# The mixture-of-experts stage of a Hyena layer: one 512-column matmul for both parts of the tokens, in 13 of 16 experts

## The chip, the cores and the metric

The kernel runs on one NeuronCore of a Trainium2 chip. The metric is the device time of one execution in microseconds (us), the median of three runs. TensorE is shown as PE (matmuls) and PEld (weight loads), VectorE as DVE, ScalarE as ACT, GpSimd as POOL, and SyncE, which issues the weight transfers, as SP.

## What is computed

One post-norm layer: a bidirectional Hyena long convolution over 2048 tokens of width 1024, then an expert-choice mixture of 16 experts. The change is in the experts alone:

```python
def _expert_choice_moe(h, w_router, w1, w3, w2):
    cap = EC_CAPACITY * T // N_EXPERTS          # 256 tokens for each expert
    aff = jax.nn.softmax((h @ w_router).astype(F32), -1)
    gate, idx = lax.top_k(jnp.swapaxes(aff, 1, 2), cap)
    xe = h[bidx, idx]
    he = jax.nn.silu(jnp.einsum('becd,edf->becf', xe, w1)) * jnp.einsum('becd,edf->becf', xe, w3)
    ye = jnp.einsum('becf,efd->becd', he, w2) * gate[..., None].astype(h.dtype)
    return jnp.zeros_like(h).at[bidx, idx].add(ye)
```

d is 1024 and f is 2048. All weights are fp32, 24 MB for an expert.

## The kernel before

Everything in fp32 is done by splitting: a number is a rounded part (h, "high") plus a remainder (l, "low"), each in a format that TensorE takes in one pass (fp32r), and a product a*b is three matmuls that add into the same place of PSUM: ah*bh, ah*bl, al*bh (`mm3`, L174, whose matmuls stand on L175, L176 and L177). In the profile's names `ab<-xh,w1h` the output is `ab`, the moving operand (streamed through the array, one column after the other) `xh`, and the stationary one (loaded first) `w1h`.

The stage of the experts is `phase_moe`. Each expert has 256 tokens. `route` (L1436) finds their indices, gathers the 256 rows (`xg`), transposes them on TensorE into PSUM (`tp`) four times 4 tiles, and splits each `tp` into `xh` (ACT, L1469) and `xl` (DVE, L1470). The 2048 hidden features are done in 16 blocks of 128: eight slices of weights (`fc`), and in each two blocks (`i`). For a slice, `load` brings w1, w3 and w2 (1 MB each) by SP's queue and `split` makes their high and low parts (ACT L1385, DVE L1386). For a block:

- `project` (L1479): 8 steps of k for w1 and 8 for w3. Each step is one `mm3` with 256 moving columns, so a block has 48 matmuls of 256 columns. w1's result and w3's are the two halves of one PSUM bank `ab` (2 buffers).
- `hidden` (L1489): Silu of the first half (ACT, L1491), times the second half (DVE, L1492), split into `hh` (ACT, L170) and `hl` (DVE, L171).
- `back` (L1498): 12 matmuls of 512 columns that add hidden times w2 into four banks `acc`. It is put off by one block: `flush` issues the `back` of block n-1 behind the `project` of block n, so that ACT and DVE have the time of a `back` and a `project` to make `hh` and `hl`.

After an expert's last block `finish` weighs the four `acc` banks (DVE, `y`, L1509) and scatters them into `accd` in HBM by an indirect DMA of POOL (L1515); `y` has one buffer, so that the second half of the tokens waits until the first half's DMA has landed.

Experts 0 to 12 run in the loop on L1570; there the framework's scheduler orders each engine's instructions. Experts 13 to 15 run in the loop on L1596 under a manual schedule (the order as written), together with `settle` (L1517), which normalises rows of `accd` that are complete and writes them out; it borrows the buffers of `xh` and `xl` for that. PSUM has 8 banks: four `acc`, two `ab`, two `tp`.

Of the kernel before, what the change touches and what calls it, by code (L numbers as in the profile page):

```python
# [12 lines left out]
F32 = mybir.dt.float32  # L13
F32R = mybir.dt.float32r
# [3 lines left out]
AF = mybir.ActivationFunctionType  # L18
# [31 lines left out]
def f_(ap):  # L50
    return ap.bitcast(F32)
# [122 lines left out]
def mm3(nc, out, ah, al, bh, bl, start=True, stop=True):  # L174
    nc.tensor.matmul(out, lhsT=ah, rhs=bh, start=start, stop=False)  # L175
    nc.tensor.matmul(out, lhsT=ah, rhs=bl, start=False, stop=False)  # L176
    nc.tensor.matmul(out, lhsT=al, rhs=bh, start=False, stop=stop)  # L177
# [1247 lines left out]
def phase_moe(tc, A, rowd, ident, ones_f, lg, R, xnd, accd, out):  # L1425
    nc = tc.nc
    tab, lo, hi, slot, spf = R.tab, R.lo, R.hi, R.slot, R.spf
    with ExitStack() as st:
# [7 lines left out]
        def route(e):  # L1436
# [4 lines left out]
            yield  # L1441
            p = ps.tile([128, 2, 33], F32, name="tp")
            idx = wk.tile([128, 2], I32, name="idx", bufs=4)
# [15 lines left out]
            yield  # L1459
            xh = wk.tile([128, 8, 256], F32R, name="xh")  # L1460
            xl = wk.tile([128, 8, 256], F32R, name="xl")
            nxt[:] = [idx, gate, xh, xl]
            for q in range(4):
                p = ps.tile([128, 2, 256], F32, name="tp")
                for i in range(2):
                    k = 2 * q + i
                    for h in range(2):
                        nc.tensor.transpose(out=p[:, i, h * 128:h * 128 + 128], in_=xg[h][:, k * 128:k * 128 + 128], identity=ident)
                nc.scalar.copy(xh[:, 2 * q:2 * q + 2], p)  # L1469
                nc.vector.tensor_tensor(xl[:, 2 * q:2 * q + 2], p, f_(xh[:, 2 * q:2 * q + 2]), OP.subtract)  # L1470
                yield
# [6 lines left out]

        def project(i, x, ws):  # L1479

            xh, xl = x
            fs = slice(i * 128, i * 128 + 128)
            p = ps.tile([128, 2, 256], F32, name="ab")
            for j in range(2):
                for k in range(8):
                    mm3(nc, p[:, j], ws[2 * j][:, k, fs], ws[2 * j + 1][:, k, fs], xh[:, k], xl[:, k], start=(k == 0), stop=(k == 7))
            return p

        def hidden(p):  # L1489
            s = wk.tile([128, 256], F32, name="s")  # L1490
            nc.scalar.activation(s, p[:, 0], AF.Silu)  # L1491
            nc.vector.tensor_tensor(s, s, p[:, 1], OP.mult)  # L1492
            hh = wk.tile([128, 256], F32R, name="hh")
            hl = wk.tile([128, 256], F32R, name="hl")
            split_const(nc, hh, s, hl)
            return hh, hl
# [19 lines left out]

        def settle(name, idx=None):  # L1517


            x = wk.tile([128, 2, 1024], F32, name=name)  # L1520
            if idx is None:
# [48 lines left out]
        for e in range(NE - 3):  # L1570
            idx, gate, *x = nxt
            acc = [[pa.tile([128, 512], F32, name=f"acc{h}{q}") for q in range(2)] for h in range(2)]
# [18 lines left out]
        with tc.manual_schedule():  # L1591
# [4 lines left out]
            for e in range(NE - 3, NE):  # L1596
                prev = acc, idx, gate
                idx, gate, *x = nxt
                acc = [[pa.tile([128, 512], F32, name=f"acc{h}{q}") for q in range(2)] for h in range(2)]
                rt = iter(()) if e == NE - 1 else route(e + 1)  # L1600
                for n in range(16):
                    fc, i = divmod(n, 2)
                    if i == 0:
                        ws, nw = nw, []
                    p = project(i, x, ws)
                    flush()
# [14 lines left out]
                    if todo:  # L1621
                        act.append(settle(todo[-2:], prev[1] if todo[0] == "-" else None))
                        next(act[-1])
# [10 lines left out]
            flush()  # L1634
            ys = [wk.tile([128, 1024], F32, name=n) for n in ("xh", "xl")]

# [130 lines left out]
```

## Time and profile before

| | |
|---|---|
| median of 3 runs | 4205.35 us (4202.3 to 4205.91) |
| the profiled execution | 4207.69 us, of which the profiled span is 4205.7 us |
| TensorE matmul, share of the span | 93% |
| mean granted TensorE clock | 0.967 of full speed |
| first matmul of the experts' blocks | at 1943.5 us of the span |
| the small matmuls of `route` (L1449) in expert 12, half-way through it | at 3673.3 us |

The profile's page gives each engine's busy time, the clock and traffic in 40 slices, the chain of work that ended last (followed back from the end through whatever released each step), and the costliest groups of instructions. Matmuls are pipelined and the ends of their records are modelled: one lasts longer in the records than the next one's start. What a matmul takes of TensorE's time is therefore the distance from its start to the next one's start, read from the timeline.

### The profile page before, as it was taken

What the parts mean: (1) busy time and instruction counts of PE and PEld (TensorE: products, weight loads), DVE (VectorE), ACT (ScalarE), POOL (GpSimd) and SP (SyncE); (2) the same over time, 40 slices, a digit from 0 to 9 for tenths busy, and PEclk for the clock granted to TensorE, in tenths of its full rate; (3) what the DMA queues carried; (4) which work ended last, traced back from release to release, by engine and by line L of the source; (5) the groups of instructions that cost most, each with busy time, mean ns of one, the idle gap of its engine ahead of it and who ended that gap; (6) DMA issues with size and microseconds to landing.
All of it is one profiled execution on the core that took longest, in us unless ns stands there. A gap on an engine that the chain in (4) does not pass through costs nothing.

```text
span 4205.7 us, 59336 instructions
## 1 busy us (share of the span) xinstructions
PE 3916.2 (93%) x23158; PEld 3360.2 (80%) x23158; DVE 2623.2 (62%) x3636; ACT 1886.3 (45%) x2609; POOL 961.1 (23%) x918
## 2 busy tenths in 40 slices
PE   6788999999998987965999999999999999999997
PEld 2445787787777776755999999999999999998996
DVE  7997444776766766876555555555555555556666
ACT  4554332334876873122444444444444444444443
POOL 4674211222332342120000000000000000005635
PEclk7999999999999999987999999999999999999999
DMA  6665445666778776543566666666566656656664
GB/s 188 189 203 177 129 153 174 206 212 194 208 208 230 208 222 205 166 165 123 189 213 201 191 190 201 200 191 201 192 209 194 204 193 209 193 171 228 225 230 166
DMA packets 648180, 815.30 MB, mean 194 GB/s; under 512 B 51411, under 2 KB 543203, under 8 KB 645596
## 3 DMA queue, kind: packets, MB, share of 16 engines
q1 hardware_dynamic: 593442, 694.82, 52.3%
q0 software_dynamic: 37472, 113.86, 9.3%
q10 hardware_dynamic: 16986, 2.83, 0.4%
q8 instruction: 182, 2.98, 0.3%
q14 instruction: 98, 0.80, 0.1%
HBM read 627.04 MB, written 133.97 MB: 181 GB/s over the span
## 4 chain that ended last, share of the span: by engine, by line
PE 74%; DVE 10%; DMA 8%; issue 4%; POOL 3%; ACT 1%; SPq 0%; POOLq 0%; DVEq 0%; ACTq 0%
PE ab L175 10%; PE ab L177 10%; PE ab L176 10%; PE acc L175 5%; PE acc L176 5%; PE acc L177 5%; PE ip L175 4%; PE ip L177 4%; PE ip L176 4%; DMA xr<-s1o 3%; PE xp L853 1%; PE op L175 1%; PE op L177 1%; PE op L176 1%; PE xp L833 1%
## 5 line engine op out<-in xcount | busy, mean ns | idle before, releaser
L177 PE MATMUL ab<-xh,w1l 128*128 128x256 f32 x2048 | 581.5, 284 | 3.2 <-DVE w1l L1386 3.0
L175 PE MATMUL ab<-xh,w1h 128*128 128x256 f32 x2048 | 582.9, 285 | 0.0
L177 PE MATMUL ab<-xh,w3l 128*128 128x256 f32 x2048 | 579.7, 283 | 0.5 <-DVE w3l L1386 0.5
L176 PE MATMUL ab<-xl,w1h 128*128 128x256 f32 x2048 | 579.8, 283 | 0.0
L176 PE MATMUL ab<-xl,w3h 128*128 128x256 f32 x2048 | 579.6, 283 | 0.0
L175 PE MATMUL ab<-xh,w3h 128*128 128x256 f32 x2048 | 579.6, 283 | 0.0
L1386 DVE TENSOR_TENSOR w2l<-w2r,w2h 128x2048 fp32r<-128x2048 f32 x126 | 297.6, 2362 | 317.6 <-ACT w2h L1385 317.6
L175 PE MATMUL acc<-w2h,hh 128*128 128x512 f32 x1024 | 405.4, 396 | 14.0 <-ACT hh L170 13.5
L176 PE MATMUL acc<-w2l,hh 128*128 128x512 f32 x1024 | 403.3, 394 | 0.0
L177 PE MATMUL acc<-w2h,hl 128*128 128x512 f32 x1024 | 400.5, 391 | 0.8 <-DVE hl L171 0.8
L175 PEld LDWEIGHTS ab<-xh,w1h 128*128 128x128 f32 x2048 | 392.5, 192 | 8.8 <-ACT xh L1469 0.3
L176 PEld LDWEIGHTS ab<-xl,w1h 128*128 128x128 f32 x2048 | 392.4, 192 | 8.6
L177 PEld LDWEIGHTS ab<-xh,w1l 128*128 128x128 f32 x2048 | 392.2, 191 | 4.2 <-DVE w1l L1386 4.2
L177 PEld LDWEIGHTS ab<-xh,w3l 128*128 128x128 f32 x2048 | 393.2, 192 | 0.9 <-DVE w3l L1386 0.9
L176 PEld LDWEIGHTS ab<-xl,w3h 128*128 128x128 f32 x2048 | 393.2, 192 | 0.0
L175 PEld LDWEIGHTS ab<-xh,w3h 128*128 128x128 f32 x2048 | 393.1, 192 | 0.0
L1492 DVE TENSOR_TENSOR s<-s,ab 128x256 f32<-128x256 f32 x256 | 106.9, 417 | 399.6 <-ACT s L1491 399.5
L1386 DVE TENSOR_TENSOR w1l<-w1r,w1h 128x2048 fp32r<-128x2048 f32 x126 | 301.0, 2389 | 69.5 <-ACT w1h L1385 69.4
L1386 DVE TENSOR_TENSOR w3l<-w3r,w3h 128x2048 fp32r<-128x2048 f32 x126 | 292.9, 2325 | 53.8 <-ACT w3h L1385 53.8
L1515 POOL DMA_INDIRECT accd<-y,idx x27 | 64.4, 2385 | 1120.2 <-DVE y L1509 1120.2
L1385 ACT CAST w2h<-w2r 128x2048 fp32r<-128x2048 f32 x128 | 244.0, 1906 | 153.3 <-PE acc L177 145.1
L1491 ACT ACTIVATE s<-ab 128x256 f32<-128x256 f32 x256 | 97.4, 380 | 448.0 <-PE ab L177 448.0
(401 smaller groups left out, 8728.1 us busy)
## 6 DMA issues: line engine op xcount, KB each, us to landing
w1r<-in_moe_w_dram SPq DMA_DIRECT2D x128, 1024.0 KB
w3r<-in_moe_w_dram SPq DMA_DIRECT2D x128, 1024.0 KB
w2r<-in_moe_w_dram SPq DMA_DIRECT2D x128, 1024.0 KB
fud<-ev SPq DMA_DIRECT2D x128, 256.0 KB
kr<-fud SPq DMA_DIRECT2D x64, 512.0 KB
mw<-in_mod_w_dram SPq DMA_DIRECT2D x96, 256.0 KB
wraw<-in_hy_w_in_dram SPq DMA_DIRECT2D x48, 512.0 KB
win<-in_c_win_dram SPq DMA_DIRECT2D x64, 256.0 KB
```

The source lines that it names most:

```text
L175: nc.tensor.matmul(out, lhsT=ah, rhs=bh, start=start, stop=False)
L176: nc.tensor.matmul(out, lhsT=ah, rhs=bl, start=False, stop=False)
L177: nc.tensor.matmul(out, lhsT=al, rhs=bh, start=False, stop=stop)
L833: nc.tensor.matmul(p[:, i], lhsT=s2[:, 2 * gp + i], rhs=r[:, i], start=True, stop=True)
L853: nc.tensor.matmul(p[:, i], lhsT=s2[:, 2 * gp + i], rhs=r[:, i], start=True, stop=True)
L1385: nc.scalar.copy(h, raw)
L1386: eng.tensor_tensor(l, raw, f_(h), OP.subtract)
L1491: nc.scalar.activation(s, p[:, 0], AF.Silu)
L1492: nc.vector.tensor_tensor(s, s, p[:, 1], OP.mult)
L1515: nc.gpsimd.indirect_dma_start(out=accd, out_offset=at(idx, h), in_=y, in_offset=None, compute_op=OP.add)
```

## The change

In experts 0 to 12 the high and the low parts of the tokens stand side by side in one tile `xs` (for each k: 256 columns high, 256 low). `project` now gives w1 and w3 a PSUM bank each. A step of k is two matmuls: the weights' high part against all 512 columns of `xs` (L1487), and the weights' low part against the 256 high columns (L1488), which adds into the first half of the bank. The two halves of a bank are then summed: ACT copies the second half to SBUF (L1490, `u0` or `u1`), DVE adds the first half (L1491). Silu (ACT, L1493) and the product of `u0` and `u1` (DVE, L1510) now read SBUF. `ab` has three buffers, and `tp` one.

Experts 13 to 15 keep the 256-column products and one bank (`project_summed`, L1497), reading both halves of `xs`. `settle` gets its buffers from a tile `xs`, which is taken at an expert's start.

```diff
@@ route
-            p = ps.tile([128, 2, 33], F32, name="tp")
+            p = ps.tile([128, 2, 33], F32, name="tp", bufs=1)
...
-            xh = wk.tile([128, 8, 256], F32R, name="xh")
-            xl = wk.tile([128, 8, 256], F32R, name="xl")
-            nxt[:] = [idx, gate, xh, xl]
+            xs = wk.tile([128, 8, 2, 256], F32R, name="xs")
+            nxt[:] = [idx, gate, xs]
             for q in range(4):
-                p = ps.tile([128, 2, 256], F32, name="tp")
+                p = ps.tile([128, 2, 256], F32, name="tp", bufs=1)
...
-                nc.scalar.copy(xh[:, 2 * q:2 * q + 2], p)
-                nc.vector.tensor_tensor(xl[:, 2 * q:2 * q + 2], p, f_(xh[:, 2 * q:2 * q + 2]), OP.subtract)
+                xh, xl = (xs[:, 2 * q:2 * q + 2, c] for c in range(2))
+                nc.scalar.copy(xh, p)
+                nc.vector.tensor_tensor(xl, p, f_(xh), OP.subtract)
                 yield
@@ project, hidden
-        def project(i, x, ws):
-
-            xh, xl = x
+        def project(i, xs, ws):
             fs = slice(i * 128, i * 128 + 128)
-            p = ps.tile([128, 2, 256], F32, name="ab")
+            out = []
+            for j in range(2):
+                p = ps.tile([128, 2, 256], F32, name="ab", bufs=3)
+                for k in range(8):
+                    nc.tensor.matmul(p, lhsT=ws[2 * j][:, k, fs], rhs=xs[:, k], start=(k == 0), stop=False)
+                    nc.tensor.matmul(p[:, 0], lhsT=ws[2 * j + 1][:, k, fs], rhs=xs[:, k, 0], start=False, stop=(k == 7))
+                u = wk.tile([128, 256], F32, name=f"u{j}", bufs=2 - j)
+                nc.scalar.copy(u, p[:, 1])
+                nc.vector.tensor_tensor(u, p[:, 0], u, OP.add)
+                if j == 0:
+                    nc.scalar.activation(u, u, AF.Silu)
+                out.append(u)
+            return out
+
+        def project_summed(i, xs, ws):
+            fs = slice(i * 128, i * 128 + 128)
+            p = ps.tile([128, 2, 256], F32, name="ab", bufs=3)
             for j in range(2):
                 for k in range(8):
-                    mm3(nc, p[:, j], ws[2 * j][:, k, fs], ws[2 * j + 1][:, k, fs], xh[:, k], xl[:, k], start=(k == 0), stop=(k == 7))
-            return p
+                    mm3(nc, p[:, j], ws[2 * j][:, k, fs], ws[2 * j + 1][:, k, fs], xs[:, k, 0], xs[:, k, 1], start=(k == 0), stop=(k == 7))
+            s = wk.tile([128, 256], F32, name="u0", bufs=2)
+            nc.scalar.activation(s, p[:, 0], AF.Silu)
+            return s, p[:, 1]
 
         def hidden(p):
-            s = wk.tile([128, 256], F32, name="s")
-            nc.scalar.activation(s, p[:, 0], AF.Silu)
-            nc.vector.tensor_tensor(s, s, p[:, 1], OP.mult)
+            s, u = p
+            nc.vector.tensor_tensor(s, s, u, OP.mult)
...
@@ settle and the last three experts
-        def settle(name, idx=None):
-            x = wk.tile([128, 2, 1024], F32, name=name)
+        def settle(x, idx=None):
...
+                free = wk.tile([128, 2, 2, 1024], F32, name="xs")
...
-                    p = project(i, x, ws)
+                    p = project_summed(i, x, ws)
...
-                        act.append(settle(todo[-2:], prev[1] if todo[0] == "-" else None))
+                        act.append(settle(free[:, todo[-1] == "l"], prev[1] if todo[0] == "-" else None))
...
-            ys = [wk.tile([128, 1024], F32, name=n) for n in ("xh", "xl")]
+            free = wk.tile([128, 2, 2, 1024], F32, name="xs")
+            ys = [free[:, h, 0] for h in range(2)]
```

The scheduler places the new instructions. Three places of the order in which instructions stand on an engine follow (name, operation, output<-inputs, size of the output).

TensorE, inside a block of experts 0 to 12, where w1's last steps are followed by w3's first; first before, then now:

```order
L177 MATMUL ab<-xh,w1l 128x256
L175 MATMUL ab<-xh,w1h 128x256
L176 MATMUL ab<-xl,w1h 128x256
L177 MATMUL ab<-xh,w1l 128x256
L175 MATMUL ab<-xh,w3h 128x256
L176 MATMUL ab<-xl,w3h 128x256
L177 MATMUL ab<-xh,w3l 128x256
```

```order
L1488 MATMUL ab<-xs,w1l 128x256
L1487 MATMUL ab<-xs,w1h 128x512
L1488 MATMUL ab<-xs,w1l 128x256
L1487 MATMUL ab<-xs,w3h 128x512
L1488 MATMUL ab<-xs,w3l 128x256
```

Three matmuls of 256 columns became one of 512 and one of 256.

VectorE, the second block of a weight slice (numbers tell the buffers apart; `w1l` and `w3l` belong to a later slice), first before, then now:

```order
L1386 TENSOR_TENSOR w2l_22754<-w2r_22743,w2h_22753 128x2048
L1386 TENSOR_TENSOR w1l_22920<-w1r_22913,w1h_22919 128x2048
L1386 TENSOR_TENSOR w3l_22924<-w3r_22915,w3h_22923 128x2048
L1492 TENSOR_TENSOR s_22732<-s_22732,ab_22671 128x256
L171 TENSOR_TENSOR hl_22736<-s_22732,hh_22735 128x256
```

```order
L1386 TENSOR_TENSOR w2l_21888<-w2r_21877,w2h_21887 128x2048
L1386 TENSOR_TENSOR w1l_22034<-w1r_22027,w1h_22033 128x2048
L1491 TENSOR_TENSOR u0_21832<-ab_21815,u0_21832 128x256
L1386 TENSOR_TENSOR w3l_22038<-w3r_22029,w3h_22037 128x2048
L1491 TENSOR_TENSOR u1_21853<-ab_21836,u1_21853 128x256
L1510 TENSOR_TENSOR u0_21832<-u0_21832,u1_21853 128x256
L171 TENSOR_TENSOR hl_21870<-u0_21832,hh_21869 128x256
```

The sum of w1's bank stands between the two weight subtractions, the sum of w3's bank behind the second, ahead of the product.

VectorE again, where `route` splits the next expert's transposed tokens, first before, then now:

```order
L1386 TENSOR_TENSOR w3l_20986<-w3r_20977,w3h_20985 128x2048
L1492 TENSOR_TENSOR s_20780<-s_20780,ab_20719 128x256
L1470 TENSOR_TENSOR xl_20788<-tp_20789,xh_20787 128x512
L171 TENSOR_TENSOR hl_20784<-s_20780,hh_20783 128x256
L1470 TENSOR_TENSOR xl_20788<-tp_20796,xh_20787 128x512
```

```order
L1386 TENSOR_TENSOR w3l_18075<-w3r_18066,w3h_18074 128x2048
L1491 TENSOR_TENSOR u1_17877<-ab_17860,u1_17877 128x256
L1470 TENSOR_TENSOR xs_17897<-tp_17898,xs_17897 128x2x256
L1510 TENSOR_TENSOR u0_17856<-u0_17856,u1_17877 128x256
L171 TENSOR_TENSOR hl_17894<-u0_17856,hh_17893 128x256
L1470 TENSOR_TENSOR xs_17897<-tp_17905,xs_17897 128x2x256
```

One operation more stands ahead of the second set's subtraction, and with one `tp` bank the second set of transposes may start only when the first set's subtraction is done. On TensorE the four sets stood, before, as two together, then 14 matmuls of `project`, the third, 4 matmuls, the fourth. Now 12 matmuls of `project` stand between the first and the second set, 9 before the third and 9 before the fourth.

## Rows read from the trace of the kernel before

**Rows 1.** the page: busy time by engine, and the chain that ended last, by engine.

```profile
PE 3916.2 (93%) x23158; PEld 3360.2 (80%) x23158; DVE 2623.2 (62%) x3636; ACT 1886.3 (45%) x2609; POOL 961.1 (23%) x918
...
PE 74%; DVE 10%; DMA 8%; issue 4%; POOL 3%; ACT 1%; SPq 0%; POOLq 0%; DVEq 0%; ACTq 0%
```

**Rows 2.** busy time by stretch: PE, PEld, DVE, ACT, POOL; clock; DMA.

```profile
2400.00:2600.00 200.00, 200.00 (x1414) 188.15 (x1413) 107.04 (x114) 87.89 (x86) 9.03 (x6) 1.00 0.60 194
...
3800.00:4205.00 405.00, 368.18 (x2527) 340.61 (x2526) 267.31 (x289) 166.97 (x174) 203.37 (x193) 0.97 0.63 213
```

**Rows 3.** the chain in order of time, 2000 to 3700 us: start, length.

```profile
2012.06 0.36 PE tp L1449 x4
...
3673.34 0.36 PE tp L1449 x4
```

**Rows 4.** TensorE's timeline in expert 7: start, length of the record.

```profile
3000.95 0.28 PE L175 MATMUL ab<-xh,w3h 128*128 128x256 f32 x1
...
3003.71 0.28 PE L177 MATMUL ab<-xh,w3l 128*128 128x256 f32 x1
3003.83 0.40 PE L175 MATMUL acc<-w2h,hh 128*128 128x512 f32 x1
...
3006.35 0.39 PE L177 MATMUL acc<-w2h,hl 128*128 128x512 f32 x1
3006.58 0.28 PE L175 MATMUL ab<-xh,w1h 128*128 128x256 f32 x1
```

**Rows 5.** TensorE's timeline in the input projection, 512 columns throughout.

```profile
440.16 0.39 PE L175 MATMUL ip<-hh,wh 128*128 128x512 f32 x1
...
442.65 0.39 PE L177 MATMUL ip<-hh,wl 128*128 128x512 f32 x1
```

**Rows 6.** TensorE's timeline in the output projection, 512 columns throughout.

```profile
1701.51 0.39 PE L176 MATMUL op<-wol,zh 128*128 128x512 f32 x1
...
1702.91 0.39 PE L176 MATMUL op<-wol,zh 128*128 128x512 f32 x1
```

**Rows 7.** ACT's timeline behind the block that ends at 3012.3 us.

```profile
3012.41 1.91 ACT L1385 CAST w3h<-w3r 128x2048 fp32r<-128x2048 f32 x1 [0.98 <-PE ab L176]
3014.23 0.37 ACT L1491 ACTIVATE s<-ab 128x256 f32<-128x256 f32 x1
```

**Rows 8.** DVE's timeline behind the same block.

```profile
3014.35 2.29 DVE L1386 TENSOR_TENSOR w3l<-w3r,w3h 128x2048 fp32r<-128x2048 f32 x1 [0.59 <-ACT w3h L1385]
3016.56 0.41 DVE L1492 TENSOR_TENSOR s<-s,ab 128x256 f32<-128x256 f32 x1
3017.45 0.42 DVE L171 TENSOR_TENSOR hl<-s,hh 128x256 fp32r<-128x256 f32 x1 [0.47 <-ACT hh L170]
```

**Rows 9.** the chain in order of time, between the experts at 2366 us.

```profile
2367.29 6.74 DMA accd<-y,idx
2374.12 0.76 DVE y L1509
```

**Rows 10.** waits of PEld, 2000 to 3780 us: total, times, longest.

```profile
PEld acc L175 <- DVE y L1509: 2.8, 7, 0.7
```

**Rows 11.** DVE's timeline where the next expert's tokens are split.

```profile
2339.29 2.29 DVE L1386 TENSOR_TENSOR w3l<-w3r,w3h 128x2048 fp32r<-128x2048 f32 x1 [0.59 <-ACT w3h L1385]
...
2341.83 0.68 DVE L1470 TENSOR_TENSOR xl<-tp,xh 128x512 fp32r<-128x512 f32 x1
```

**Rows 12.** ACT's timeline there.

```profile
2343.26 0.59 ACT L1469 CAST xh<-tp 128x512 fp32r<-128x512 f32 x1 [0.91 <-PE tp L1468]
```

**Rows 13.** TensorE's timeline there: first two sets of transposes, then the third.

```profile
2340.02 1.03 PE L1468 MATMUL tp<-ident,xg 128*128 128x128 f32 x8
...
2342.57 0.66 PE L1468 MATMUL tp<-ident,xg 128*128 128x128 f32 x4
```

**Rows 14.** TensorE's timeline, the first expert's transposes.

```profile
1941.89 1.75 PE L1468 MATMUL tp<-ident,xg 128*128 128x128 f32 x7 [1.73 <-DMA xg<-xnd,idx]
...
1946.01 1.05 PE L1468 MATMUL tp<-ident,xg 128*128 128x128 f32 x4
```

More of the change, by code (lines that the diff above doesn't have):

```diff
@@ L1570, in phase_moe @@
         for e in range(NE - 3):
-            idx, gate, *x = nxt
+            idx, gate, x = nxt
             acc = [[pa.tile([128, 512], F32, name=f"acc{h}{q}") for q in range(2)] for h in range(2)]
@@ L1597, in phase_moe @@
                 prev = acc, idx, gate
-                idx, gate, *x = nxt
+                idx, gate, x = nxt
+                free = wk.tile([128, 2, 2, 1024], F32, name="xs")
                 acc = [[pa.tile([128, 512], F32, name=f"acc{h}{q}") for q in range(2)] for h in range(2)]
```

## The prediction

> **What bounds the kernel now.** I read the page's busy times first. TensorE (PE) is busy for 93% of the span, and the chain that ended last stands on it for 74% [rows 1]. An average over stages says little, so the stretches come next. In experts 0 to 12 PE is busy without a gap at full clock, while VectorE (DVE) is busy for 54% and ScalarE (ACT) for 44%; only behind 3800 us, in the last three experts, which the change leaves on their old products, do gaps open [rows 2]. The chain in order of time has the same mark (the two small matmuls of L1449) once an expert: 12 periods between 2012.06 and 3673.34 us, 138.44 us each [rows 3].
>
> What fills them is read from the timeline, by distances between starts. From the first w3 matmul to the last it is 23 steps in 2.76 us: 120 ns for a matmul of 256 columns. The 12 matmuls of `back`, 512 columns each, take from 3003.83 to 3006.58 us: 229 ns each [rows 4]. So a block costs 48 x 0.120 + 12 x 0.229 = 8.51 us, 16 blocks 136.2 us, and the transposes and L1449 the other 2.2 us: the stage is TensorE's order of instructions and nothing else. A matmul saved there is time saved, until something else becomes late.
>
> **Where the saving comes from.** The change streams as many columns as before (512 + 256 in place of 3 x 256), with 32 matmuls in place of 48. It can gain only if a matmul costs something beyond its columns. The rows say that it does: two of 256 columns take 240 ns, one of 512 takes 229 ns in `back` [rows 4], 11 steps in 2.49 us = 226 ns in the input projection [rows 5], and 6 steps in 1.40 us = 233 ns in the output projection [rows 6]. No row before has 512 and 256 columns by turns over a stretch. Two junctions do: the last 512 ahead of a 256 takes 0.23 us (3006.35 to 3006.58), the last 256 ahead of a 512 takes 0.12 us (3003.71 to 3003.83) [rows 4]. I take 227 ns for the 512, since in the input projection, as in the new step, tokens move and weights stand, and 120 ns for the 256. A pair is then 347 ns where three took 360: 13 ns less. Bounds: 226 ns and 233 ns for the 512 give 14 and 7 ns.
>
> There are 13 experts x 16 blocks x 2 products x 8 steps = 3328 pairs. 3328 x 13 ns = **43.3 us less** (23 to 47 by the bounds).
>
> The trace makes the cost beside the columns some 13 ns a matmul: 120 and 227 ns against 107 and 213 ns for the columns alone at 2.4 GHz, the level granted there [rows 2]. The Trainium skill has a smaller one, in "TensorE: Matmul & The Clock Gate", section "Back-to-back issue gap": N / 2.4 + 2.5 ns for an isolated matmul. By that a pair would save 2.5 ns, an estimate of 8.3 us in all, and the sum below would end near 4203 us, the third rival's case. Its 109 ns for 256 columns is not what this trace shows (120 ns) [rows 4]; the sum goes by the trace.
>
> **What is added, and what covers it.** A block gets two copies on ACT and two sums on DVE. The nearest rows are Silu from the same PSUM tile (0.37 us) [rows 7] and the product that reads it (0.41 us) [rows 8]. Per weight slice (two blocks, 17 us) ACT goes from 3 x 1.91 + 2 x 0.78 = 7.3 to 8.8 us, DVE from 3 x 2.29 + 2 x 0.83 = 8.5 to 10.2 us: neither becomes the bound. I take nothing for it; the cover is that `hh` and `hl` are wanted one `back` and one `project` later.
>
> That cover is thinnest behind the second block of a slice, where w3's cast and subtraction stand ahead. Before, from the cast's start at 3012.41 us [rows 7] to the end of `hl` at 3017.87 us [rows 8] it is 5.46 us. Now the copy takes Silu's place beside the subtraction, and the sum adds 0.42 us behind it: 5.9 us. TensorE wants it after a `back` (2.75 us) and a `project` (16 x 0.347 = 5.55 us), 8.3 us. So 2.4 us are left. The three `ab` banks are freed sooner still.
>
> **What gets later.** Three small terms, all from the thirteen experts.
>
> - Between experts, the second `y` waits for the first one's DMA, 6.74 us, and TensorE waits for that `y` [rows 9]. In 7 cases TensorE's queue waits already [rows 10]. The DMA starts from an `acc` that TensorE has finished, and one `project` lies between, now 16 x 13 ns = 0.21 us shorter. 7 x 0.21 = 1.5 us lost (0 to 12 x 0.21 = 2.5).
> - `route` with one `tp` bank. Before, the third set waited for the first set's subtraction: that ended at 2342.51 us, 3.22 us behind the start of w3's subtraction [rows 11], and the set began at 2342.57 [rows 13]. Now the second set does, with the sum in the product's place, so at the same 3.22 us. TensorE comes to it 0.73 us (2340.02 against 2339.29) + 0.40 us (four transposes) + 12 matmuls (2.08 us) = 3.21 us behind the same start: level. For the third and fourth set a round is ACT's copy 0.59 us [rows 12], the subtraction 0.68 us [rows 11], and an operation of `hidden` on each engine in front (0.41 us each), 2.1 us; TensorE brings 0.4 us of transposes and 9 matmuls, 1.6 us: 2.0 us. I take 0.25 us an expert, 12 x 0.25 = 3.0 us. Bounds: 0, and a round that nothing covers, 3 x 1.4 us x 12 = 50 us.
> - The first expert's `route` runs with little to hide it. Before, the first seven of eight transposes ran in one go and the last set started at 1946.01 us, 4.1 us behind the first [rows 14]. With one bank each of three sets waits for copy and subtraction, 1.3 us, partly beside matmuls of the first block. I take 1.4 us (0 to 4).
>
> Nothing is taken for experts 13 to 15: their matmuls, their wait for Silu and the settling of rows stand in the order they had, and the borrowed tile is free from the expert before, as its two forerunners were.
>
> **The sum:** -43.3 + 1.5 + 3.0 + 1.4 = -37.4 us. The profiled execution took 4207.69 us (span 4205.7 us), 2.3 us over the median; taken from it, 4170.3 us; taken from the median of 4205.35 us, **4168.0 us**. About 0.2%, 8.4 us, is what a measurement can tell from no change.
>
> **The rivals.**
>
> 1. *`hidden` comes late (slower).* Its place is the second block of each slice: 104 of them. It decides once the chain of 5.9 us goes beyond 8.3 us, by 0.36 us for the gain to be gone and by 0.44 us to be slower. One more weight part on ACT and DVE ahead of the sum (1.91 + 2.29 us) would make it 10.1 us: 1.8 us x 104 = 187 us, 4355 us. For it: in the last three experts TensorE does wait for `hh`. Against it: the order now has the sum directly behind w3's subtraction, and 2.4 us are left. Chance 5%.
> 2. *The transposes' rounds lie open (no gain or slower).* With the 50 us above in place of 3.0 us: 4215 us. It decides where each set waits its whole round; rows 11 to 13 have them level. Chance 3%; half of it (25 us, 4190 us, still faster) 6%.
> 3. *Columns set the time.* If the mixed pair takes 358 to 360 ns, the gain is 0 to 8 us and the later terms remain: 4203 to 4211 us, no change. For it: no stretch of the trace has the mix, and a weight load might cost more behind a matmul of another length. Against it: both junctions. Chance 7%.
> 4. *A bigger gain.* If with 512 columns the cost beside them vanishes in the next load (512 at 216 ns, the 256 at 120): 24 ns a pair, 80 us, 4131 us. No 512 in rows 4 to 6 is that short. Chance 3%.
> 5. *The change does not do what it says.* The order shows 16 + 16 matmuls a block in the thirteen experts, so I give it nothing.
>
> **How the numbers follow.** The forecast has 76%. Its own range is 4168 - 8 (14 ns a pair, nothing lost beyond the 1.5 us) to 4168 + 20 (7 ns a pair): 4160 to 4188 us. The range for 8 in 10 adds the half case of rival 2 above and something towards rival 4: **4154 to 4192 us**. Faster by over 0.2%: 76 + 6 (half of rival 2) + 3 (rival 4) + 1 of rival 3 = 86%. The same: 6 of rival 3 and 1 of rival 2 = 7%. Slower: 5 (rival 1) and 2 of rival 2 = 7%.
>
> **What would show it.** In the changed profile: steps of 227 and 120 ns by turns in `ab`; the mark of L1449 every 135.5 us (138.44 - 256 x 0.013 + 0.25 + 0.12); PE busy without a gap through experts 1 to 12; waits of PE for `hh` none there, for `y` some 4 us in all, and for `xs` of `route` up to 0.3 us a set; the time behind 3800 us as long as before, only earlier. I am wrong if the period is 138 us (pairs of 360 ns), or if `acc` waits for ACT in each slice.

## The result, and the profile after

The changed kernel takes 4176.29 us (median of 6 runs, 4171.81 to 4184.32), the kernel before beside it 4203.83 us (6 runs): a ratio of 0.9938, 95% interval 0.9925 to 0.9951. That is 27.5 us faster where 37.4 us were forecast: the sign and the order of size are right, a quarter of the gain is missing.

The page of the changed kernel still has TensorE as the bound, with fewer instructions (19830 for 23158), and DVE and ACT busier by about 157 and 140 us [rows 1]:

```profile
PE 3884.4 (93%) x19830; PEld 3170.8 (76%) x19830; DVE 2780.4 (67%) x4052; ACT 2026.8 (49%) x3025; POOL 963.0 (23%) x918
```

Busy time by stretch (PE, PEld, DVE, ACT, POOL, each with its instructions; granted clock; DMA share; GB/s). Experts 0 to 12 stay without a gap at full clock, with 1062 matmuls in these 200 us for 1414 [rows 2]:

```profile
2400.00:2600.00 200.00, 200.00 (x1062) 170.58 (x1061) 124.59 (x161) 103.23 (x134) 9.26 (x6) 1.00 0.61 198
```

The chain in order of time (start, length) has the mark of L1449 at:

```profile
2005.28 0.37 PE tp L1449 x4
...
3643.28 0.37 PE tp L1449 x4
```

Twelve periods in 1638.00 us are **136.50 us** each, against 138.44 before [rows 3] and 135.5 forecast: 1.94 us an expert. With this the 31.6 us between the two profiled spans are accounted for: 12 x 1.94 = 23.3 us here; 1.6 us behind the last mark (4174.1 - 3643.28 = 530.8 us, before 532.4); 0.2 us between the first expert's own mark (1926.56, before 1933.18) and the first of these; and 6.6 us ahead of that mark, where no edit is. In the runs below that start moves by 13 us from profile to profile. So the code gave some 25 us (23.3 + 1.6 + 0.2), and medians of two versions can differ by a few us that the edit did not cause. The period leaves the start out, and I compare by it.

Where the quarter went is seen on TensorE's timeline (start, length of the record, line):

```profile
2411.80 0.40 PE L175 MATMUL acc<-w2h,hh 128*128 128x512 f32 x1
...
2414.54 0.53 PE L1449 MATMUL tp<-tab,oh 128*128 128x33 f32 x4
...
2415.34 0.39 PE L1487 MATMUL ab<-xs,w1h 128*128 128x512 f32 x1
2415.57 0.28 PE L1488 MATMUL ab<-xs,w1l 128*128 128x256 f32 x1
2415.69 0.40 PE L1487 MATMUL ab<-xs,w1h 128*128 128x512 f32 x1
2415.93 0.28 PE L1488 MATMUL ab<-xs,w1l 128*128 128x256 f32 x1
...
2417.46 0.40 PE L1487 MATMUL ab<-xs,w1h 128*128 128x512 f32 x1
...
3069.20 0.40 PE L175 MATMUL acc<-w2h,hh 128*128 128x512 f32 x1
```

The 12 matmuls of `back` take 2.74 us, as before. From the 512 at 2415.34 to the one at 2417.46 it is six pairs in 2.12 us: **353 ns a pair** where 347 was taken. The 256 costs 0.12 us as forecast; the 512 costs 0.23 to 0.24. Three matmuls of 256 were 360 ns, so once the turns have settled a pair saves not 13 but 6.7 ns. Over a whole block the saving is 7.1 ns a pair, since the first pair is cheaper: by distances between starts, a `project` that nothing interrupts took 5.752 us before (mean of 163) and takes 5.639 us now (mean of 165).

Waits of PEld there (total us, times, longest), 2020 to 3640 us; PE itself waits for nobody:

```profile
PEld tp L1467 <- DVE xs L1470: 4.7, 24, 0.2
PEld acc L175 <- DVE y L1527: 0.6, 3, 0.2
```

And the chain behind the second block of a slice: DVE's timeline, then ACT's (start, length; in brackets the idle time before):

```profile
3062.85 2.29 DVE L1386 TENSOR_TENSOR w3l<-w3r,w3h 128x2048 fp32r<-128x2048 f32 x1 [0.21 <-ACT w3h L1385]
3065.05 0.42 DVE L1491 TENSOR_TENSOR u<-ab,u 128x256 f32<-128x256 f32 x1
3065.58 0.42 DVE L1510 TENSOR_TENSOR u<-u,u 128x256 f32<-128x256 f32 x1
3066.47 0.43 DVE L171 TENSOR_TENSOR hl<-u,hh 128x256 fp32r<-128x256 f32 x1 [0.47 <-ACT hh L170]
```

```profile
3060.90 1.91 ACT L1385 CAST w3h<-w3r 128x2048 fp32r<-128x2048 f32 x1 [0.66 <-PE ab L1487]
```

From the cast's start to the end of `hl` it is 3066.90 - 3060.90 = 6.0 us (forecast 5.9), until TensorE begins the `back` that wants it (3069.20, the last row of its timeline above) 8.3 us (forecast 8.3).

### The profile page after: what moved, and what is told of

Its sections match the earlier page's. It is cut to its first block, busy times and chain, and to the rows that moved or that the text cites. A ratio compares the mean times of both kernels' runs of the same rounds, so it can differ in the third digit from the quotient of the medians.

```text
span 4174.1 us, 53525 instructions
## 1 busy us (share of the span) xinstructions
PE 3884.4 (93%) x19830; PEld 3170.8 (76%) x19830; DVE 2780.4 (67%) x4052; ACT 2026.8 (49%) x3025; POOL 963.0 (23%) x918
## 4 chain that ended last, share of the span: by engine, by line
PE 74%; DMA 9%; DVE 9%; POOL 3%; issue 3%; ACT 1%; SPq 1%; POOLq 0%; ACTq 0%; DVEq 0%
PE ab L1487 19%; PE ab L1488 9%; PE acc L175 5%; PE acc L176 5%; PE acc L177 5%; PE ip L175 4%; PE ip L177 4%; PE ip L176 4%; DMA xr<-s1o 3%; DMA kr<-fud 2%; PE xp L853 2%; PE ap L870 1%; PE op L175 1%; PE op L177 1%; PE op L176 1%
## 5 line engine op out<-in xcount | busy, mean ns | idle before, releaser
L1487 PE MATMUL ab<-xs,w3h 128*128 128x512 f32 x1664 | 600.4, 399 | 0.0
L1487 PE MATMUL ab<-xs,w1h 128*128 128x512 f32 x1664 | 598.1, 399 | 0.0
L1488 PE MATMUL ab<-xs,w3l 128*128 128x256 f32 x1664 | 468.2, 281 | 0.0
L1488 PE MATMUL ab<-xs,w1l 128*128 128x256 f32 x1664 | 466.6, 280 | 0.0
L1487 PEld LDWEIGHTS ab<-xs,w3h 128*128 128x128 f32 x1664 | 313.0, 188 | 76.5
L1487 PEld LDWEIGHTS ab<-xs,w1h 128*128 128x128 f32 x1664 | 312.9, 188 | 72.8
L1488 PEld LDWEIGHTS ab<-xs,w1l 128*128 128x128 f32 x1664 | 314.2, 189 | 7.1
L1488 PEld LDWEIGHTS ab<-xs,w3l 128*128 128x128 f32 x1664 | 314.7, 189 | 0.0
L1491 DVE TENSOR_TENSOR u<-ab,u 128x256 f32<-128x256 f32 x416 | 174.5, 420 | 205.6 <-ACT u L1490 197.1
L1385 ACT CAST w1h<-w1r 128x2048 fp32r<-128x2048 f32 x128 | 244.4, 1910 | 80.9 <-PE ab L1487 78.9
L1385 ACT CAST w3h<-w3r 128x2048 fp32r<-128x2048 f32 x128 | 244.7, 1911 | 68.3 <-PE ab L1487 66.3
L1490 ACT COPY u<-ab 128x256 f32<-128x256 f32 x416 | 153.1, 368 | 185.5 <-PE ab L1488 185.4
```

What stands on the lines that cost most here:

```text
L1385: nc.scalar.copy(h, raw)
L1487: nc.tensor.matmul(p, lhsT=ws[2 * j][:, k, fs], rhs=xs[:, k], start=(k == 0), stop=False)
L1488: nc.tensor.matmul(p[:, 0], lhsT=ws[2 * j + 1][:, k, fs], rhs=xs[:, k, 0], start=False, stop=(k == 7))
L1490: nc.scalar.copy(u, p[:, 1])
L1491: nc.vector.tensor_tensor(u, p[:, 0], u, OP.add)
```

## The experiments

All are made from the changed kernel and measured beside the kernel before. Period is the distance of the expert marks of L1449, first to last of 13, over 12, in the profiled run (before: 138.44 us; the change: 136.50 us). The recorded expectations count the experts from 1: their experts 1-13 are experts 0 to 12 above.

| run | median us | ratio to before, 95% | period us |
|---|---|---|---|
| all eights | 4169.18 | 0.9911 (0.9898 to 0.9925) | 135.59 |
| by sixteens | 4193.61 | 0.9972 (0.9961 to 0.9983) | 137.89 |
| copies and sums only | 4205.78 | 1.0002 (0.9993 to 1.0011) | 138.57 |
| two `tp`, two `ab` banks | 4175.05 | 0.9929 (0.9914 to 0.9945) | 136.48 |
| by twos | 4163.69 | 0.9908 (0.9895 to 0.9922) | 135.30 |
| lagged lows | 4174.44 | 0.9928 (0.9914 to 0.9941) | 136.28 |
| by sixteens, `y` apart | 4162.56 | 0.9899 (0.9884 to 0.9914) | 135.05 |
| all eights, also in the last three | 4185.27 | 0.9951 (0.9938 to 0.9965) | 135.57 |
| the change, `y` apart | 4181.09 | 0.9943 (0.9931 to 0.9955) | 136.47 |
| four more on the chain | 4194.10 | 0.9974 (0.9961 to 0.9987) | 137.73 |
| eight more on the chain | 4212.61 | 1.0023 (1.0013 to 1.0033) | 138.87 |

**All eights.** Is it the order, or the lengths? The same matmuls, not by turns:

```diff
 for k in range(8):
     nc.tensor.matmul(p, lhsT=ws[2 * j][:, k, fs], rhs=xs[:, k], start=(k == 0), stop=False)
+for k in range(8):
     nc.tensor.matmul(p[:, 0], lhsT=ws[2 * j + 1][:, k, fs], rhs=xs[:, k, 0], start=False, stop=(k == 7))
```

> Within each product the eight 512-column matmuls come first, then the eight of 256; nothing else differs. Theory A (the cost beside the columns is per matmul, and what is missing of the forecast gain is lost where the two lengths alternate): a product goes from 2820 ns to about 2800 ns (8 x 227 + 8 x 120, and some 30 ns for the first 512s behind 256s, as in back), 416 ns... that is 20 ns x 2 x 208 blocks = 8 us less than the change, about 4168 us. Theory B (columns set the time, 0.46 ns each, in any order once the lengths are mixed): 2820 ns stay, the time is that of the change, 4176 us.

TensorE's timeline of this run, one block (x8: eight matmuls):

```profile
2413.79 1.98 PE L1487 MATMUL ab<-xs,w1h 128*128 128x512 f32 x8
2415.60 1.11 PE L1489 MATMUL ab<-xs,w1l 128*128 128x256 f32 x8
2416.55 2.00 PE L1487 MATMUL ab<-xs,w3h 128*128 128x512 f32 x8
2418.39 1.12 PE L1489 MATMUL ab<-xs,w3l 128*128 128x256 f32 x8
2419.35 0.40 PE L175 MATMUL acc<-w2h,hh 128*128 128x512 f32 x1
```

Eight 512s take 1.81 and 1.84 us (226 and 230 ns each), eight 256s 0.95 and 0.96 us (119 and 120 ns): the two prices of the prediction, but for the 512s that stand behind 256s. The block's 16 pairs take 5.56 us (16 x 347 ns = 5.55), the period is 135.59 us (forecast 135.5): Theory A. The prices were right; turning between them at every matmul cost the 6 ns.

**By sixteens.** One more step that way: both products' 512s, then both products' 256s, so that the sums come later, one behind the other.

```diff
+banks = []
 for j in range(2):
     p = ps.tile([128, 2, 256], F32, name="ab", bufs=3)
+    banks.append(p)
     for k in range(8):
         nc.tensor.matmul(p, lhsT=ws[2 * j][:, k, fs], rhs=xs[:, k], start=(k == 0), stop=False)
+for j in range(2):
+    p = banks[j]
+    for k in range(8):
         nc.tensor.matmul(p[:, 0], lhsT=ws[2 * j + 1][:, k, fs], rhs=xs[:, k, 0], start=False, stop=(k == 7))
```

> All sixteen 512-column matmuls of a block (w1, then w3) come first, then the sixteen of 256, so that the back of the block before (512 columns) runs into them and only one change of length each way is left in a block. Theory A (lost by alternation): project and back together go from 8.39 us a block to 28 x 0.227 + 16 x 0.120 = 8.28 us and a little for the change of length, some 8.30 us: 0.085 us x 208 = 18 us less than the change, about 4158 us. Theory B (columns set the time): 4176 us, a block stays 8.39 us. Both: the w1 bank is summed 2 us later, inside the 2.3 us that the chain to hl has left, so no new wait.

Against both theories it is slower than the change. The waits of PE, 2020 to 3640 us, have a new one, once an expert:

```profile
PE acc L177 <- DVE hl L171: 22.5, 12, 2.0
```

DVE's timeline in front of one of them:

```profile
2092.60 2.29 DVE L1386 TENSOR_TENSOR w2l<-w2r,w2h 128x2048 fp32r<-128x2048 f32 x1 [1.95 <-ACT w2h L1385]
2097.02 1.41 DVE L1532 SCALAR_TENSOR_TENSOR y<-acc,gate,m 128x512 f32<-128x512 f32 x2 [2.13 <-DMA accd<-y,idx]
2098.35 0.42 DVE L171 TENSOR_TENSOR hl<-u,hh 128x256 fp32r<-128x256 f32 x1
```

`hh` was done long before (ACT's row below); `hl` could have followed at 2094.9 us. But the built order of DVE has the second `y` ahead of it, which stands 2.13 us until the first `y`'s DMA has read the shared buffer. TensorE starts again at 2098.82 us, after 1.97 us idle:

```profile
2092.47 0.40 ACT L170 CAST hh<-u 128x256 fp32r<-128x256 f32 x1
2098.82 0.50 PE L177 MATMUL acc<-w2h,hl 128*128 128x512 f32 x1 [1.97 <-DVE hl L171]
```

**By sixteens, `y` apart.** The test of that reading: give the second `y` the buffer of `xg0`.

```diff
-pend.append(partial(finish, acc, idx, gate))
+pend.append(partial(finish, acc, idx, gate, ("y", "xg0")))
```

> The order by sixteens again (both products' 512s, then both products' 256s), but the two halves of y at an expert's end have two buffers (y and xg0, as the last three experts already have them), so that VectorE need not wait for the first half's transfer before it writes the second. In the trace by sixteens VectorE's queue holds the weighing of the second half ahead of hl, 2.1 us idle until the transfer of the first half has read the buffer, and TensorE waits 1.9 to 2.0 us for hl once per expert, and in five of twelve periods loses 1.7 us more while the granted clock is down. Theory A (the slower time by sixteens is that one queued wait): it goes, the period falls from 137.0 to 138.8 us to 135.6 us and the time from 4193.6 to 4169 us (4166 to 4172). Theory B (with both sums behind one another hl comes too late anyway): at least half of the loss stays, 4181 us or more.

DVE's timeline at the same place:

```profile
2086.46 1.40 DVE L1532 SCALAR_TENSOR_TENSOR y<-acc,gate,m 128x512 f32<-128x512 f32 x2
2087.78 1.40 DVE L1532 SCALAR_TENSOR_TENSOR xg<-acc,gate,m 128x512 f32<-128x512 f32 x2
...
2090.15 2.29 DVE L1386 TENSOR_TENSOR w2l<-w2r,w2h 128x2048 fp32r<-128x2048 f32 x1 [0.64 <-ACT w2h L1385]
2092.36 0.42 DVE L171 TENSOR_TENSOR hl<-u,hh 128x256 fp32r<-128x256 f32 x1
```

The wait is gone (PE waits for nobody in the thirteen experts), the period is 135.05 us and the time 4162.56 us, lower than Theory A's range. TensorE's timeline says why it beats the eights: the second run of 512s no longer stands behind 256s.

```profile
2096.29 1.98 PE L1489 MATMUL ab<-xs,w1h 128*128 128x512 f32 x8
2098.10 1.98 PE L1489 MATMUL ab<-xs,w3h 128*128 128x512 f32 x8
2099.91 1.12 PE L1493 MATMUL ab<-xs,w1l 128*128 128x256 f32 x8
2100.87 1.12 PE L1493 MATMUL ab<-xs,w3l 128*128 128x256 f32 x8
2101.83 0.40 PE L175 MATMUL acc<-w2h,hh 128*128 128x512 f32 x1
```

Eight 512s in 1.81, eight 256s in 0.96 us, twice. 13 x (138.44 - 135.05) = 44 us off: the 43.3 us of the first term, whole. By the period it is the fastest version here; the time is 1.0% below the kernel before.

**The change, `y` apart**, the control for it: the same line alone.

> The change as it is, with the two halves of y at an expert's end in two buffers, as in the run by sixteens with y apart: the control for that run. Theory A (in the change the weighing of y holds nobody up: TensorE waits 0.6 us for it in all): no difference, 4176 us (4173 to 4179), period 136.5 us. Theory B (part of what that run gained is due to y alone): 4172 us or less.

Period 136.47 us, as the change. The median is 5 us above the change's and above Theory A's range, but the intervals of the two ratios overlap, and in the profile the first expert mark stands 7 us later than in the change's. Theory A, by the period; `y` gains nothing where nobody waits for it.

**By twos.** How many matmuls of one length in a row are enough?

```diff
-for k in range(8):
-    nc.tensor.matmul(p, lhsT=ws[2 * j][:, k, fs], rhs=xs[:, k], start=(k == 0), stop=False)
-    nc.tensor.matmul(p[:, 0], lhsT=ws[2 * j + 1][:, k, fs], rhs=xs[:, k, 0], start=False, stop=(k == 7))
+for k0 in range(0, 8, 2):
+    for k in (k0, k0 + 1):
+        nc.tensor.matmul(p, lhsT=ws[2 * j][:, k, fs], rhs=xs[:, k], start=(k == 0), stop=False)
+    for k in (k0, k0 + 1):
+        nc.tensor.matmul(p[:, 0], lhsT=ws[2 * j + 1][:, k, fs], rhs=xs[:, k, 0], start=False, stop=(k == 7))
```

> Experts 1-13 as in the change, but each product issues two 512-column matmuls, then the two 256-column matmuls of the same two chunks, and so on: per product a 512 follows a 256 four times (with the one before the product), where it is eight times in the change and once with all eights together. Theory A (each 512 that follows a 256 costs TensorE a fixed few ns): the loss against all eights shrinks in that proportion, three sevenths of it are left; the period of an expert should be 136.0 us (all eights 135.6, the change 136.5) and the time 4172 us (4170 to 4174). Theory B (only a single 256 between two 512s is dear, as the pattern of three pairs in the change suggests): 135.6 us and 4169 us. Theory C (only the grouping of a whole product helps): 136.5 us and 4176 us.

TensorE's timeline (x2: two matmuls):

```profile
2413.00 0.63 PE L1488 MATMUL ab<-xs,w1h 128*128 128x512 f32 x2
2413.47 0.39 PE L1490 MATMUL ab<-xs,w1l 128*128 128x256 f32 x2
2413.70 0.63 PE L1488 MATMUL ab<-xs,w1h 128*128 128x512 f32 x2
...
2415.78 0.63 PE L1488 MATMUL ab<-xs,w3h 128*128 128x512 f32 x2
```

From 2413.00 to 2415.78 it is eight pairs in 2.78 us: 347 to 348 ns a pair. The two 512s cost more (0.47 us, 233 ns each), the two 256s give it back (0.23 us, 115 ns each). Period 135.30 us: Theory B. A fixed price for each change of length, Theory A, falls: with four changes a product the loss against all eights is not three sevenths but nil. What is dear is to turn at every matmul. By whole blocks (means of 165 to 168 that nothing interrupts) a `project` takes 5.639 us by turns, 5.564 by twos, 5.560 by eights and 5.539 by sixteens with `y` apart. That the period by twos is 0.29 us shorter than by eights comes from `back`, 2.741 us for 2.760, and not from the products.

**Lagged lows.** By turns as in the change, but the 256 takes chunk k-1, so that no two neighbours read the same tokens.

```diff
-for k in range(8):
-    nc.tensor.matmul(p, lhsT=ws[2 * j][:, k, fs], rhs=xs[:, k], start=(k == 0), stop=False)
-    nc.tensor.matmul(p[:, 0], lhsT=ws[2 * j + 1][:, k, fs], rhs=xs[:, k, 0], start=False, stop=(k == 7))
+for k in range(9):
+    if k < 8:
+        nc.tensor.matmul(p, lhsT=ws[2 * j][:, k, fs], rhs=xs[:, k], start=(k == 0), stop=False)
+    if k > 0:
+        nc.tensor.matmul(p[:, 0], lhsT=ws[2 * j + 1][:, k - 1, fs], rhs=xs[:, k - 1, 0], start=False, stop=(k == 8))
```

> As the change, strictly alternating 512 and 256 columns, but the 256-column matmul behind the 512 of chunk k takes chunk k-1, so that it no longer reads the rows of tokens that the matmul just before it read. Theory A (the alternation of lengths costs, whatever is read): 136.5 us a period and 4176 us (4174 to 4178), as the change. Theory B (reading the same tokens twice in a row costs): 135.6 us a period and 4169 us.

Period 136.28 us: Theory A. Reading the same tokens twice in a row is not what costs. The 0.2 us below the change need not be the tokens either: in this order each product begins with two 512s and ends with two 256s, which no longer stand by turns.

**Copies and sums only.** All that the change adds, without what it removes: 48 matmuls of 256 columns, with the change's banks, copies and sums.

```diff
 for k in range(8):
-    nc.tensor.matmul(p, lhsT=ws[2 * j][:, k, fs], rhs=xs[:, k], start=(k == 0), stop=False)
+    nc.tensor.matmul(p[:, 1], lhsT=ws[2 * j][:, k, fs], rhs=xs[:, k, 1], start=(k == 0), stop=(k == 7))
+for k in range(8):
+    nc.tensor.matmul(p[:, 0], lhsT=ws[2 * j][:, k, fs], rhs=xs[:, k, 0], start=(k == 0), stop=False)
     nc.tensor.matmul(p[:, 0], lhsT=ws[2 * j + 1][:, k, fs], rhs=xs[:, k, 0], start=False, stop=(k == 7))
```

> The change with 48 matmuls of 256 columns a block as before (the low part of the tokens into the second half of each bank, the rest into the first half); the copies, the sums, the banks and the one transposing bank are the change's. Theory A and B: project is back at 5.75 us a block and the added work is hidden, so the time is that of the kernel before and 1 to 5 us for the transposes: 4204 to 4209 us. Rival (the copies and sums cost TensorE time through waits, and ate part of the gain): clearly over 4212 us.

No difference from the kernel before. 416 copies of 0.37 us and 416 sums of 0.42 us are hidden, and the whole gain is TensorE's. The run also answers a rival to the lengths: that it is the change between high and low weights that costs. In the second loop of each product the weights go by turns here too, at one length, and the step stays 120 ns:

```profile
2503.50 0.28 PE L1489 MATMUL ab<-xs,w1h 128*128 128x256 f32 x1
2503.62 0.28 PE L1490 MATMUL ab<-xs,w1l 128*128 128x256 f32 x1
```

That takes out the weights. The change from a whole bank to half a bank always goes with the length and is not tested apart from it.

**Two `tp`, two `ab` banks**, at all four places of the stage:

```diff
-name="tp", bufs=1
+name="tp", bufs=2
-name="ab", bufs=3
+name="ab", bufs=2
```

> The change with two banks for tp and two for ab, as before. If three ab banks are needed, TensorE waits for the sum of a bank in the second block of each slice, over 0.2 us x 104, and it is slower than the change by 20 us or more. By the rows of the changed kernel (the sum of the w3 bank ends 4.6 us behind that product, its bank is wanted again 5.6 us behind it) two are enough: no such wait, the waits of the transposes (5 us in all) go, and it is 1 to 5 us faster than the change, 4171 to 4176 us.

Period 136.48 us to the change's 136.50, and TensorE waits for nobody in either: between experts the single `tp` bank costs nothing, and the third `ab` bank serves nothing. At the first expert there is a difference: from its own mark (1924.08 us here) to the next (2001.93 us) it is 77.9 us, and 78.7 us in the change.

**All eights, also in the last three experts.** From the kernel with all eights:

```diff
-p = project_summed(i, x, ws)
+p = project(i, x, ws)
```

> The order by eights, and the last three experts use it too (512 columns, copy and sum) in place of 48 matmuls of 256 columns. Theory A (TensorE's matmuls set the time there too): 768 pairs at 13 ns, 10.0 us, come off, and up to 5 us more where the low half of w1 is waited for, since it is wanted later: 4156 us (4153 to 4161). Theory B (there the hidden values are already waited for, 12.3 us in nine places, and each such place gets the copy and the sum, some 0.9 us, added): the gain is eaten in part, 4162 to 4169 us.

Slower than all eights by 16 us, where Theory B, the worse of the two, gave 4169 us at most. The waits of PE, 3640 to 4190 us, have a line that the run with all eights hasn't:

```profile
PE ab L1487 <- DVE u L1492: 27.1, 8, 7.7
```

TensorE waits for a bank that DVE has not read. DVE's timeline ahead of the longest (the sum starts at 3919.89; ACT's copy for it was done by 3908.8 us):

```profile
3901.39 3.06 DVE L1511 TENSOR_TENSOR u<-u,u 128x256 f32<-128x256 f32 x1
...
3906.88 4.50 DVE L1386 TENSOR_TENSOR w1l<-w1r,w1h 128x2048 fp32r<-128x2048 f32 x1
...
3919.89 0.42 DVE L1492 TENSOR_TENSOR u<-ab,u 128x256 f32<-128x256 f32 x1
```

With one bank a block, three banks carry three blocks; with two, one and a half, and a sum 11 us late in DVE's queue stops TensorE for 7.7 us. The product is part of what makes DVE late: it now reads two tiles in SBUF, and where POOL works beside it, it takes 0.67 to 3.06 us (15 times), while with one operand in PSUM, in the last three experts of all eights, it kept 0.41 to 0.42 us in all 15. That the last three experts kept one bank was right.

**Four, and eight, more on the chain.** How much slack has the chain to `hl`? In the second block of each slice of experts 0 to 12, m operations `u = max(u, u)` on DVE:

```diff
 nc.vector.tensor_tensor(u, p[:, 0], u, OP.add)
+if i == 1 and j == 1:
+    for _ in range(m):
+        nc.vector.tensor_tensor(u, u, u, OP.max)
```

> The change, and in every second block of experts 1-13 four VectorE operations of 128x256 (u = max(u, u), some 0.45 us from start to start) between the second product's sum and the product u*u: the chain to hl gets 1.8 us longer. The trace of the change has 6.0 us of chain against 8.3 us until TensorE wants hl, 2.3 us left. Theory A (that slack is as read): no wait on TensorE, 4176 us (4173 to 4182). Theory B (the chain is already nearly late): TensorE waits for hl in 104 blocks, 1 us each or more: 4280 us or above.

> The same with eight such operations: 3.6 us more on the chain, 1.3 us beyond the slack. As the program is built, TensorE's order moves seven matmuls of the next block's product, some 1.2 us, ahead of the output projection there. Theory A (slack and order together): the wait is covered but for a few tenths of a us in 104 blocks: 4176 to 4215 us. Theory B (the order covers nothing): 1.3 us x 104 = 135 us: 4311 us. Theory C (VectorE's queue gets late and with it the sums that free the banks): well above that, 4400 us or more.

With four, the waits of PE, 2020 to 3640 us:

```profile
PE acc L175 <- ACT hh L170: 11.5, 12, 1.1
```

With eight:

```profile
PE acc L175 <- DVE y L1530: 16.6, 12, 2.3
```

In both PE waits at one place an expert, not eight: the first blocks of the next expert, behind `y`. With four, DVE's timeline there has the second `y` behind 1.85 us for the first one's DMA, and everything behind it later:

```profile
2094.05 1.41 DVE L1530 SCALAR_TENSOR_TENSOR y<-acc,gate,m 128x512 f32<-128x512 f32 x2 [1.85 <-DMA accd<-y,idx]
```

So the 2.3 us hold for the ordinary blocks (Theory A there), but not for this one, and the 4194 us lie outside Theory A's range. That the wait would go with `y` apart is read from the timeline; no run shows it. With eight, the 4213 us are at the upper end of Theory A, far from B and C: the scheduler of the build had moved seven matmuls of the next product ahead of `back`. DVE's queue late at `y` is the larger part of what is left, but not all of it: PE's waits are 1.4 us of the 2.4 us that a period got longer. In ordinary blocks the weight loads wait now as well (PEld for `hh` 33 times, 0.4 us at most, and for `hl` 36 times, 0.2 us), and the rest I can put to no row.

## Why the prediction came out as it did

**The bound: right.** TensorE without a gap, everything added hidden: copies and sums alone change nothing, and the waits of PE stay empty.

**The first term, -43.3 us: mis-sized, the step that failed.** It is 3328 pairs x 13 ns, and it took the two prices from stretches of one length and from two junctions [rows 4, 5]. For stretches of one length each was right: all eights and by sixteens have 227 and 120 ns. What failed is the step from there to the mix: a stretch by turns settles at 353 ns, 3328 x 6.7 = 22.3 us, just below the lower bound (7 ns, 23 us) that I had kept, from a 512 of 233 ns. The two junctions had been read on the wrong side, at the matmul ahead of the change of length. The one behind it shows more, and it stood in the same timeline of before: from the 512 at 3003.83 us [rows 4] to the next it is 0.24 us, and then 0.23.

```profile
3004.07 0.40 PE L176 MATMUL acc<-w2l,hh 128*128 128x512 f32 x1
3004.30 0.39 PE L177 MATMUL acc<-w2h,hl 128*128 128x512 f32 x1
```

Over the 163 blocks of before the first two 512s of a `back` take 233 and 236 ns on average, the last five 227, and the first 256 of a `project` gives some of it back (114 ns for 120). So the trace of before had a 512 of 233 ns for just this case; what a stretch by turns settles at, it could not have told. "No row before has 512 and 256 columns by turns" was there and should have moved the value off the end that suited the forecast. Grouped by sixteens the term comes whole (44 us).

**The losses, +5.9 us: mostly not there.** The single `tp` bank was given 3.0 us between experts: the weight loads waited 24 times, 0.2 us at most, and PE never; with two banks the period is the same. `y` was given 1.5 us: PEld's wait for it fell from 2.8 us [rows 10] to 0.6 us. The first expert's start was given 1.4 us: eight blocks before its next mark should have saved 8 x 0.12 = 1.0 us and saved 0.2, so some 0.8 us was lost; with two `tp` banks the 1.0 us is there (77.9 us for 78.9), which puts the loss to the single bank, by one profile of each. The losses were given too much and the gain too much: two errors of opposite sign, so that by luck the forecast was off by 10 us rather than 16.

**The chain to `hl`: right in an ordinary block** (6.0 of 8.3 us), **blind at the expert's start**, where four operations more (1.8 us) were enough to make TensorE wait.

**Rival 1, `hidden` comes late:** not in the change, but its mechanism is real: by sixteens and with four or eight more on the chain TensorE waits for `hh`, `hl` or `y`. Its price was wrong. It strikes once an expert (12 times 1 to 2 us), where the `y` that waits for a DMA stands ahead in DVE's queue, not in all 104 blocks. Eight operations more put 3.6 of its 4.2 us on the chain and gave 4213 us, not 4355; with a whole weight part ahead of the sum there is no run.

**Rival 2, the transposes:** no trace of it. **Rival 3, columns set the time:** nearer than its 7% by the number, the pair at 353 ns lying half way from 347 to its 358 to 360, but not by its mechanism: in another order the same columns take 347 ns and less. The Trainium skill, "TensorE: Matmul & The Clock Gate", section "Back-to-back issue gap", has N / 2.4 + 2.5 ns for an isolated matmul. By that a matmul saved is worth 2.5 ns, an estimate. By sixteens with `y` apart one is worth 13 ns (44 us over 3328), by turns 6.7 ns; the trace does not agree with it in either. **Rival 4, a bigger gain:** eight 512s in a row take 226 ns each at the least, not 216.

**Still open:** what in TensorE makes lengths by turns dear. Shown is that in runs of two or more the cost is gone or nearly so (5.564 us a `project` for 5.539 at the least), and that neither the tokens read nor the turn from high to low weights is it. The 0.2 us an expert between 256 x 6.7 ns = 1.72 and the measured 1.94 us are in the blocks: 16 x (5.752 - 5.639) = 1.81 us in `project`, and 0.19 us in `back`, which takes 2.748 us on average for 2.760.

## What to carry to other kernels

Where matmuls of two lengths share a loop, put equal lengths together, two in a row at least: here merging them by turns brought 25 us (13 x 1.94), two by two 41 us (13 x 3.14). A price read at a junction of two stretches is not the price of their mix, and at a junction the matmul behind it has to be read, not only the one ahead; where no row has the mix, take the cautious end. And before an order is made that gives results later, look for what stands ahead in the engines' queues: by sixteens a `y` waiting for a DMA cost 2.8 us a period (137.89 for 135.05), more than the 1.4 us that the matmuls' order gave, and one buffer removed it.

## What the runs showed of the hardware that I had not expected

A 512 behind 256s is dearer than one in a long run, and a 256 behind 512s is cheaper. In the second product of all eights the first five 512s behind the 256s take 233, 236, 228, 233 and 231 ns (means over 168 blocks), the rest 227; the first 256 behind them takes 113 ns, the next 119, the rest 120. By turns it settles to a pattern of three pairs, 233 and 117, 241 and 120, 236 and 113 ns, 353 a pair. Two by two the 256s give back what the 512s cost (115 ns for 120), by turns they don't. A change of length is not all that makes a 512 dear: in the output projection, 512 columns throughout, one takes 233 ns [rows 6].

DVE operations with two operands in SBUF took twice as long and more while POOL multiplied or added large tiles [the rows of all eights in the last three]: `w1l` 4.50 us instead of 2.29, the product 3.06 instead of 0.42. The sum, which reads PSUM and SBUF, kept its 0.41 to 0.43 us in all 26 cases that fell beside such an operation. An operation with one large operand and a column of scalars in SBUF (L1439, at 3756.07 us of that run) was held up too, 2.49 us instead of 0.35. POOL's timeline in the stretch of `w1l` and the product:

```profile
3901.74 2.41 POOL L1567 TENSOR_TENSOR xs<-xs,gb 128x1024 f32<-128x1024 f32 x1
...
3909.30 4.30 POOL L1568 TENSOR_TENSOR xs<-xs,gb 128x1024 f32<-128x1024 f32 x1
```

That agrees with the Trainium skill, "SBUF — State Buffer", section "SBUF: two separate sides": a VectorE operation with two SBUF inputs and a GpSimd operation that reads SBUF lock a shared pair of ports against each other.

By sixteens, the wait of 2 us for `hl` sometimes cost more than itself. Busy time by stretch behind the waits of two experts (the number ahead of the last two is the granted clock):

```profile
2098.00:2104.00 6.00, 5.18 (x16) 4.09 (x17) 6.00 (x7) 0.42 (x1) 3.68 (x1) 0.72 0.50 166
2237.00:2243.00 6.00, 5.35 (x24) 4.43 (x24) 6.00 (x7) 0.42 (x1) 3.70 (x1) 1.00 0.53 168
```

In the first the clock fell to the lower level (1.2 GHz) for a while, with starts of 512 columns 0.43 us apart (2100.69 and 2101.12 us) in place of 0.23; in the second, behind as long a wait, it did not. Of the twelve periods five are some 1.7 us longer than the rest. These five have a mean granted clock of 0.99, the other seven 1.00. With four and with eight more on the chain, where PE waits 0.8 to 2.3 us once an expert, no such fall shows: the granted clock from 2020 to 3640 us is 1.00 in both.
